# A transformer block with conditioning, state space, attention and product-key experts: features by quarters, conditioning on TensorE beside the gates, value tiles in turn

## The chip, the cores and the metric

The kernel runs on one core of a Trainium2 chip. The metric is the device time of one execution in microseconds, as a median over runs. TensorE multiplies matrices, VectorE and ScalarE work element by element, GpSimd (POOL in the profile) does so too and issues the indirect transfers, SyncE (SP) issues most of the others. Sixteen DMA engines move data between HBM and the on-chip memory.

## What is computed

256 tokens of width 2048 go through one block, in float32. The conditioning vector `c` gives six rows of 2048 (shift, scale and gate of both halves), by one product with a 2048 x 12288 matrix.

```python
s1, sc1, g1, s2, sc2, g2 = split(silu(c) @ w_ada + b_ada, 6)
h = rmsnorm(x, norm1_g) * (1 + sc1) + s1
u, q, kv, gates = split(h @ w_in)            # 2048 -> 1024, 1024, 1536, 24
y = concat(rmsnorm(s5_mixer(u)) * beta_ssm, rmsnorm(nsa_attention(q, kv, gates)) * beta_attn)
x = x + g1 * (y @ w_out)
h2 = rmsnorm(x, norm2_g) * (1 + sc2) + s2
x = x + g2 * peer(h2)
return rmsnorm(x, final_g)

def peer(h):             # 16384 experts; 8 heads choose 16 each per token
    expert, gate = top16_of_products(h @ w_q, sub_k1, sub_k2)
    a = gelu(h @ exp_u[expert].T)
    return (gate * a) @ exp_v[expert]
```

(`rmsnorm(v, g)` stands for the norm and its weight; the reference writes these lines out.) Products must keep float32 accuracy.

## The kernel before

**Split products.** A float32 weight unit of 128x1024 (512 KB) is loaded into one of four raw buffers (`unit`, L79), rounded by ScalarE to a `hi` part and its rest `lo` taken by VectorE (`split`, L89). Each product is then three fast ones: hi with hi, hi with lo, lo with hi. There are two buffers for each part in the later stages.

**Order.** The builder writes the work in program order; a planner with a timeline of its own then places each engine's instructions, by priority and by when operands should be ready. An engine carries out its own list strictly in order, and so does each engine's list of transfers to issue. `issue_after` pins an instruction behind another, `high_priority` moves a group up.

**Front.** The weights of the conditioning come in units of one 128-row tile and 1024 columns. `cond_job` (L379) multiplies 16 units of one half of one row group with `silu(c)`, in four column groups of the array side by side, and `cond_end` (L401) turns the summed rows into columns with small products (`pscol`, L415). The halves of `h` (`h_half`, L430) take the conditioning of scale (j = 1) and shift (j = 0). The first half is loaded through 11 buffers before anything is projected; then 16 projection blocks (`win_block`, L511) with the first half of the depth run, mixed with the second half's conditioning through a ring of three buffers `adap`, and `h_half(1)` follows. Meanwhile GpSimd builds the tables of the state space mixer.

**Middle.** A plan of blocks (L475 to L510, each with a cost) does the rest of the projections, the recurrence and the compression, then heads, gated projection and output projection. `pump` (L452) puts in steps of the conditioning of g1, scale and shift of the second norm: one per 8 of planned cost (L872), then in `tick` (L972) at every second tick, from the 17th at every one. There are 48 steps of two units. The results are turned into columns `late = 6` pumps after a job's end. `h2` is formed from products with a diagonal matrix (L1022) and the conditioning columns.

**Experts.** All 16384 experts are computed: 128 up-projection tiles (`u_tile`, L1067) of two units and 48 products each give activations of 128 experts by 256 tokens in `SA` (88 tiles) and `SB` (40). Beside the first 25 the top-16 choice runs; the next 64 are mixed with `g_group` (L1186), two per tile, which builds the gates of two tokens from one-hot rows: VectorE makes them, GpSimd scales them, TensorE multiplies, and VectorE and GpSimd multiply them into the activations. Then each expert's row of 256 weights, with its number in column 256, is scattered (88 indirect transfers, L1302) to HBM, in the order of places (`places`, L1242): experts that only the first 128 tokens use, that both use, that only the second use. In the same loop `g2_job` (L1307) computes g2: 32 units, one VectorE multiply-add each (L1315), summed over partitions by four products at the end.

**Value tiles.** `todo` (L1464) lists 51 places of the first list and 23 of the second, in order. `ENDS` says which hold which token tile: 20 for the first only, 15 for both, 16 for the second only; in the second list 8, 7 and 8. `load_rows` (L1357) loads the sorted weights four tiles at a time (514 KB, two buffers), and gathers the 128 rows of `peer_v` (1 MB) through their indices into one of four buffers. `v_tile` (L1426) splits rows and weights and runs 12 products of 512 columns for each token tile. From the fifth tile on, one scatter of the second list follows each tile, 40 in all. At `turn` all engines meet for a branch (L1494) that handles counts outside `ENDS`. `finals` (L1435) scales by g2, adds and normalizes.

Of the kernel before, what the change touches and what calls it, by code (L numbers as in the profile page):

```python
# [8 lines left out]
F32 = mybir.dt.float32  # L9
# [32 lines left out]

POOL_PAIRS = (1, 5, 9, 13)
# [7 lines left out]
ENDS = ((20, 35, 51), (8, 15, 23))  # L51


def build(tc, A):
# [34 lines left out]
    def split(raw, n=1024, lo_engine=None):  # L89

        hi, lo = buf("hi"), buf("lo")
        nc.scalar.copy(hi[:, :n], raw[:, :n])  # L92
# [100 lines left out]
    hT, uT, qT = uq, uq[:, :8], uq[:, 8:]  # L193
# [159 lines left out]

    for tt in range(2):
# [6 lines left out]
        norm_transpose(hv, ss[:, 2:3], s5t, lambda k, ps, tt=tt: nc.scalar.copy(  # L361
            hT[:, k:k + 4, tt * 128:(tt + 1) * 128], ps), "pqs",
            lambda: psS.tile([128, 4, 128], F32, name="pst", tag="py", bufs=2))
# [10 lines left out]
    sel2 = base1.tile([128, 2], F32, name="sel2")  # L374
    nc.vector.memset(sel2, 0.0)
    for i in range(4):
        nc.vector.memset(sel2[32 * i:32 * i + 1, i % 2:i % 2 + 1], 1.0)

    def cond_job(j, h, tags, late=0):  # L379
        ps = psM.tile([128, 512], F32, name="cps", tag="cps", bufs=1)  # L380
        for kt in range(0, KT, 2):
            rs = []
            for k in (kt, kt + 1):
                p, tag, bufs = tags[k % len(tags)]
                src = A["w_ada"][k * 128:(k + 1) * 128, j * D + h * 1024:j * D + (h + 1) * 1024]
                rs.append(unit(src, p, tag, bufs))
            for g in range(4):
                k, q = kt + g // 2, g % 2
                nc.tensor.matmul(ps[32 * g:32 * g + 32, :], scz[:, k], rs[g // 2][:, q * 512:(q + 1) * 512],  # L389
                                 start=kt == 0, stop=kt == KT - 2)  # L390
            yield
        rows = base1.tile([128, 512], F32, name="rows", tag="rows", bufs=1)
        nc.scalar.copy(rows, ps)
        if late:
            finish.append([late, j, h, rows])
        else:
            cond_end(j, h, rows)
# [3 lines left out]
    def cond_end(j, h, rows):  # L401
        if j == 2:
            b = base1.tile([1, 1024], F32, name="row", tag="adap", bufs=3)
            nc.gpsimd.dma_start(b, A["b_row"][0:1, h * 1024:(h + 1) * 1024])
            for q in range(2):
                cs = slice(q * 512, (q + 1) * 512)
                ps = psM.tile([1, 512], F32, name="psr", tag="mm", bufs=1)
                nc.tensor.matmul(ps, sel2[:, q:q + 1], rows, start=True, stop=True)
                nc.vector.tensor_tensor(out=b[:, cs], in0=b[:, cs], in1=ps, op=OP.add)
            nc.gpsimd.dma_start(g1d[:, h * 1024:(h + 1) * 1024], b)  # L410
        else:
            i = {0: 0, 1: 1, 3: 2, 4: 3}[j]
            ps = psM.tile([128, 8], F32, name="pscol", tag="mm", bufs=1)
            for b in range(8):
                nc.tensor.matmul(ps[:, b:b + 1], rows[:, b % 4 * 128:(b % 4 + 1) * 128], sel2[:, b // 4:b // 4 + 1],  # L415
                                 start=b == 0, stop=b == 7)
            o = cond[:, i, 8 * h:8 * h + 8]
            nc.vector.tensor_tensor(out=o, in0=ps, in1=bada[:, j, 8 * h:8 * h + 8], op=OP.add)
            if j in (1, 4):
                nc.vector.scalar_tensor_tensor(o, o, 1.0, ng[:, j // 4, 8 * h:8 * h + 8],  # L420
                                               op0=OP.add, op1=OP.mult)
# [8 lines left out]
    def h_half(h):  # L430
# [1205 lines left out]
```

## Time and profile before

| | us |
|---|---|
| three runs | 1933.39, 1949.06, 3670.4 |
| median | 1949.06 |
| the profiled execution | 1938.97 |
| its span, first to last instruction | 1937.2 |

| busy in the span | TensorE | VectorE | ScalarE | GpSimd |
|---|---|---|---|---|
| us | 1780.6 | 1440.4 | 798.2 | 788.6 |
| share | 92% | 74% | 41% | 41% |

The DMA engines move 440.39 MB, 227 GB/s on average. Busy time of TensorE overlaps itself, since products are pipelined and their ends are modelled: its pace is better read from the number of products in a stretch. The mean granted TensorE clock is 0.964 of full speed. The stages by time: conditioning and first norm to 172 us, middle to 560, output projection and second norm to 668, top-16 choice to 918, gates to 1337, maxima for the places to 1410, scatters to 1610, value tiles to the end.

### The profile page before, as it was taken

To read this page: it belongs to the slowest core of one execution; us is meant where nothing else is said; L and a number is where in the kernel's file an instruction comes from. 1 tells how busy PE (TensorE), PEld (TensorE's weight loads), DVE (VectorE), ACT (ScalarE), POOL (GpSimd) and SP (SyncE) were. 2 spreads that over 40 slices of the span, in tenths; PEclk is the share of its full clock that TensorE was granted. 3 is DMA by queue.
4 is the path that set the end of the run, shared out by engine and by line. 5 is a ranking of instruction groups with operands and counts; after the bars stand their busy time and mean duration, and the time that the engine had idled before them with its cause. 6 is when DMAs were issued, how large, how long until landed. Compare 5 with 4: busy or idle time off the path is not lost. (4 is left out here: it accounts for less than half of the span.)

```text
span 1937.2 us, 32031 instructions
## 1 busy us (share of the span) xinstructions
PE 1780.6 (92%) x11928; PEld 1492.2 (77%) x11928; DVE 1440.4 (74%) x2716; ACT 798.2 (41%) x1286; POOL 788.6 (41%) x867
## 2 busy tenths in 40 slices
PE   5798999999999799999999999999988888899896
PEld 2475666567776499999999999999977886687674
DVE  2524998856754288888999999999866666756657
ACT  3222222148633244344444444444323334645554
POOL 5910333201001101111766677774056744756333
PEclk8799999999999899999999999999989998999998
DMA  9769457587658455555555555445589996978974
GB/s 384 275 221 331 168 173 255 186 293 252 223 191 295 159 180 176 184 174 162 161 169 164 164 161 156 158 155 164 181 271 293 291 358 244 365 274 276 360 284 163
DMA packets 115994, 440.39 MB, mean 227 GB/s; under 512 B 16037, under 2 KB 18789, under 8 KB 105846
## 3 DMA queue, kind: packets, MB, share of 16 engines
q1 hardware_dynamic: 89712, 322.41, 50.1%
q0 software_dynamic: 21968, 112.29, 16.0%
q10 hardware_dynamic: 4150, 3.56, 0.6%
q8 instruction: 96, 1.57, 0.3%
q14 instruction: 68, 0.56, 0.1%
HBM read 415.05 MB, written 23.15 MB: 226 GB/s over the span
## 5 line engine op out<-in xcount | busy, mean ns | idle before, releaser
L92 ACT CAST hi<-raw 128x1024 fp32r<-128x1024 f32 x385 | 403.3, 1048 | 708.1 <-PE pa L471 316.4
L93 DVE TENSOR_TENSOR lo<-raw,hi 128x1024 fp32r<-128x1024 f32 x382 | 517.3, 1355 | 197.9 <-ACT hi L92 180.2
L471 PE MATMUL pa<-hhi,lo 128*128 128x256 f32 x2048 | 592.3, 289 | 38.3 <-DVE lo L93 37.5
L471 PE MATMUL pa<-hhi,hi 128*128 128x256 f32 x2048 | 584.6, 285 | 7.5 <-ACT hi L92 7.3
L471 PE MATMUL pa<-hlo,hi 128*128 128x256 f32 x2048 | 583.7, 285 | 0.0
L471 PEld LDWEIGHTS pa<-hhi,lo 128*128 128x128 f32 x2048 | 396.1, 193 | 54.0 <-DVE lo L93 51.5
L471 PEld LDWEIGHTS pa<-hhi,hi 128*128 128x128 f32 x2048 | 396.3, 193 | 8.9 <-ACT hi L92 8.9
L471 PEld LDWEIGHTS pa<-hlo,hi 128*128 128x128 f32 x2048 | 396.4, 194 | 0.0
L1402 DVE TENSOR_TENSOR lv<-rv,hv 128x1024 fp32r<-128x1024 f32 x144 | 174.4, 1233 | 79.2 <-ACT hv L1401 78.3
L1200 POOL TENSOR_TENSOR mv<-o,gp 128x256 fp32r<-128x256 f32 x256 | 168.6, 679 | 121.6 <-DVE o L1197 95.6
L1401 ACT CAST hv<-rv 128x1024 fp32r<-128x1024 f32 x144 | 147.6, 1049 | 95.5 <-DMA rv<-in_peer_v,wt 47.2
L1197 DVE TENSOR_TENSOR o<-pT,iota 128x256 fp32r<-128x256 f32 (+1 forms) x256 | 160.7, 629 | 1.4 <-PE pgs L1203 1.0
L389 PE MATMUL cps<-adap,scz 128*32 128x512 f32 x544 | 133.1, 651 | 23.2 <-DMA adap<-in_w_ada 23.2
L471 PE MATMUL lin<-hhi,hi 128*128 128x256 f32 x480 | 143.1, 299 | 3.9 <-ACT hhi L1034 2.1
L471 PE MATMUL lin<-hlo,hi 128*128 128x256 f32 x480 | 140.3, 293 | 6.4 <-DVE hlo L438 5.1
L471 PE MATMUL lin<-hhi,lo 128*128 128x256 f32 x480 | 140.0, 292 | 0.0
L1218 POOL TENSOR_TENSOR SA<-SA,gs 128x50 f32<-128x50 f32 (+42 forms) x128 | 134.3, 1050 | 1.4 <-DVE gs L1211 1.4
L1371 POOL DMA_INDIRECT rv<-in_peer_v,wt x74 | 88.7, 1198 | 103.3 <-DVE lv L1402 53.8
L1302 POOL DMA_INDIRECT wc<-SA,slot x88 | 105.5, 1199 | 47.4 <-DVE slot L1294 23.0
L471 PEld LDWEIGHTS lin<-hhi,hi 128*128 128x128 f32 x480 | 93.8, 196 | 33.4 <-issue 21.8
L1118 POOL TENSOR_TENSOR eq<-eq,iff 128x512 f32<-128x512 f32 x16 | 30.0, 1896 | 212.4 <-DVE eq L1117 212.4
L471 PEld LDWEIGHTS lin<-hlo,hi 128*128 128x128 f32 x480 | 93.7, 195 | 19.8 <-issue 9.9
(433 smaller groups left out, 3053.3 us busy)
## 6 DMA issues: line engine op xcount, KB each, us to landing
raw<-in_peer_u SPq DMA_DIRECT2D x256, 512.0 KB, 3.5
adap<-in_w_ada SPq DMA_DIRECT2D x136, 512.0 KB, 4.8
raw<-in_w_in SPq DMA_DIRECT2D x48, 512.0 KB, 5.6
raw<-in_w_out SPq DMA_DIRECT2D x32, 512.0 KB, 4.3
raw<-in_peer_wq SPq DMA_DIRECT2D x32, 512.0 KB, 3.5
raw<-in_w_ada SPq DMA_DIRECT2D x32, 512.0 KB, 5.8
wt<-wc POOLq DMA_DIRECT2D x19, 514.0 KB, 6.7
raw<-in_cmp_w SPq DMA_DIRECT2D x16, 512.0 KB, 4.4
```

Of the source, the lines that this page charges most:

```text
L92: nc.scalar.copy(hi[:, :n], raw[:, :n])
L93: (lo_engine or nc.vector).tensor_tensor(out=lo[:, :n], in0=raw[:, :n], in1=hi[:, :n].bitcast(F32), op=OP.subtract)
L389: nc.tensor.matmul(ps[32 * g:32 * g + 32, :], scz[:, k], rs[g // 2][:, q * 512:(q + 1) * 512], start=kt == 0, stop=kt == KT - 2)
L471: nc.tensor.matmul(ps, w, a[:, kk], start=first and u == 0 and k == 0 and i == 0, stop=last and u == n - 1 and k == 7 and i == 2)
L1118: nc.gpsimd.tensor_tensor(out=eq, in0=eq, in1=bc(iff[:, half].unsqueeze(2), EQ), op=OP.mult)
L1197: nc.vector.tensor_tensor(out=o, in0=bc(pT[:, j, t:t + 2].unsqueeze(2), shp), in1=io, op=OP.is_equal)
L1200: nc.gpsimd.tensor_tensor(out=mv[:, :, j], in0=o2, in1=g, op=OP.mult)
L1218: nc.gpsimd.tensor_tensor(out=o, in0=o, in1=tmp[:, a0:m], op=OP.mult)
L1302: d = nc.gpsimd.indirect_dma_start(out=wcs[i], out_offset=bass.IndirectOffsetOnAxis(ap=ap, axis=0), in_=SB[:, m - NSA] if i else SA[:, m], ...
L1371: d = nc.gpsimd.indirect_dma_start(out=raw, out_offset=None, in_=A["peer_v"], in_offset=bass.IndirectOffsetOnAxis(ap=t[:, T:T + 1].bitcast ...
L1401: nc.scalar.copy(hi, raw)
L1402: nc.vector.tensor_tensor(out=lo, in0=raw, in1=hi.bitcast(F32), op=OP.subtract)
```

## The change

**Front.** The conditioning weights are laid out so that a unit holds 2 depth tiles by 512 columns, whole in HBM. `cond_job` now does a quarter of a row group (8 units), with one vector `sel4` in place of `sel2`. `h_quarter` replaces `h_half`; features 4 to 7 of the depth go to two tiles of their own. The first quarter's conditioning is 16 units. The 16 projection units then hold two blocks by four depth tiles each (`win_quarter`, weights `w_inq`), eight for the first quarter and eight for the second, with 26 steps of the other three quarters' conditioning between them. Two loads of the mixer move behind the twelfth of them.

**Pump.** The later conditioning is done in quarters too, a step per 6 of planned cost and one at every tick, and is turned into columns 2 pumps after its end.

**g2.** Its 32 units are loaded beside the gates, two at every fourth up-projection tile, and multiplied on TensorE with one column of `silu(c)`, in four column groups. `g2_end` adds the bias and stores the row. The multiply-adds and loads beside the scatters go.

**Value tiles.** The index column moves to column 128, between the two token tiles' weights, so the columns of one token tile and the index lie together. Each tile loads its own weights: 129 of 257 columns if one token tile needs them, 257 if both; six buffers. The order is `ORDER_A` and `ORDER_B`. The gelu and multiply of an up-projection tile beside the gates become two instructions where they cross column 128. Indices of the second list's scatters are made one at a time, each behind the last row split. The first six row and three weight casts are pinned behind the last up-projection cast. The first token tile's `finals` comes one tile after its last product, with three more tiles to go.

```diff
+EARLY = (1, 1, 1, 2, 1, 2, 1, 1), (2, 2, 2, 2, 2, 2, 2, 2)
+ORDER_A = "0000" + "0b1" * 15 + "01"
+ORDER_B = "00b001" * 2 + "bb1bb1b11" + "11"
+TURN = 12
...
+    def cond_job(j, q, tags, late=0):
         ps = psM.tile([128, 512], F32, name="cps", tag="cps", bufs=1)
-        for kt in range(0, KT, 2):
+        for kt in range(0, KT, 4):
             rs = []
+            for p2 in (kt // 2, kt // 2 + 1):
+                p, tag, bufs = tags[p2 % len(tags)]
+                rs.append(unit(A["w_ada"][j, q, p2], p, tag, bufs))
             for g in range(4):
+                nc.tensor.matmul(ps[32 * g:32 * g + 32, :], scz[:, kt + g],
+                                 rs[g // 2][:, g % 2 * 512:(g % 2 + 1) * 512], start=kt == 0, stop=kt == KT - 4)
...
-    ada = jobs(((2, 0), (2, 1), (4, 0), (4, 1), (3, 0), (3, 1)), ring, 6)
+    ada = jobs([(j, q) for j in (2, 4, 3) for q in range(4)], ring, 2)
...
+    def parts():
+        for q in range(1, 4):
+            for j in (1, 0):
+                yield from cond_job(j, q, ring)
+            h_quarter(q)
+    steps = parts()
+    for q in range(2):
+        for b in range(8):
+            win_quarter(b, outs[b], q)
+            for _ in range(EARLY[q][b]):
+                next(steps, None)
+            if (q, b) == (1, 3):
+                s5_load()
+                s5_craw(0)
...
-        for _ in range(int(spent / 8) - int(x0 / 8)):
+        for _ in range(int(spent / 6) - int(x0 / 6)):
             pump(1)
...
-        pump(1 if clock[0] % 2 or clock[0] > 16 else 0)
+        pump(1)
...
+    def g2_job():
+        for kt in range(KT):
+            rs = [unit(A["w_g2"][kt * 128:(kt + 1) * 128, h * 1024:(h + 1) * 1024])
+                  for h in range(2)]
+            for g in range(4):
+                nc.tensor.matmul(g2ps[32 * g:32 * g + 1, :], scol[:, kt:kt + 1],
+                                 rs[g // 2][:, g % 2 * 512:(g % 2 + 1) * 512], start=kt == 0, stop=kt == KT - 1)
+            yield
...
+    g2 = g2_job()
     while state["t"] < T:
         for _ in range(2):
             g_group()
+        if state["t"] % 16 == 0:
+            next(g2, None)
         u_tile()
...
-                if kt:
-                    nc.vector.scalar_tensor_tensor(ac, r, sc, ac, op0=OP.mult, op1=OP.add)
...
-            chunks[i, c] = pool.tile([128, 4, T + 1], F32, name="wt", tag="wt" + tag, bufs=1 if tag else 2)
+        wt = pool.tile([128, T + 1], F32, name="wt", tag="wt" + tag, bufs=2 if tag else 6)
+
+        cs = slice(128 if tts[0] else 0, T + 1 if tts[-1] else 129)
+        nc.gpsimd.dma_start(wt[:, cs], wcs[i][128 * j:128 * j + 128, cs])
         raw = pool.tile([128, D], F32, name="rv", tag="rv" + tag, bufs=2 if tag else 4)
...
-    todo = [(i, j) for i in range(2) for j in range(ENDS[i][2])]
+    todo = []
+    for i, order in enumerate((ORDER_A, ORDER_B)):
+        of = {k: [j for j in range(ENDS[i][2]) if tts_of(i, j) == t] for k, t in zip("0b1", ((0,), (0, 1), (1,)))}
+        todo += [(i, of[k].pop(0)) for k in order]
+    turn = len(ORDER_A) + TURN
...
-        if j == ENDS[1][1] + 1:
+        if todo[turn + n - 1] == (1, ENDS[1][1] - 1):
             finals(0)
```

## Rows read from the trace of the kernel before

**Rows 1.** Table of stages (from:to in us; busy us and instructions per engine; clock; DMA; GB/s)
```profile
0.00:80.00 80.00, 44.40 (x216) 19.15 (x217) 32.89 (x93) 22.51 (x38) 58.34 (x96) 0.77 0.91 355
172.00:560.00 388.00, 377.86 (x2373) 266.99 (x2372) 309.63 (x656) 149.92 (x288) 84.57 (x91) 0.98 0.66 224
918.00:1337.00 419.00, 407.74 (x3319) 398.13 (x3319) 415.55 (x828) 196.52 (x385) 297.45 (x384) 1.00 0.50 160
1410.00:1610.00 200.00, 167.07 (x1238) 159.17 (x1237) 125.39 (x147) 64.28 (x83) 117.73 (x103) 0.94 0.92 307
1610.00:1821.00 211.00, 191.35 (x788) 149.80 (x787) 137.28 (x180) 113.45 (x148) 124.00 (x104) 0.96 0.85 300
```

**Rows 2.** Timeline of the front (start, us, engine, line, operation; what ended the idle time)
```profile
64.09 3.57 PE L415 MATMUL pscol<-sel,rows 128*128 128x1 f32 x16 [0.74 <-ACT rows L393]
...
67.90 8.50 DVE L435 TENSOR_SCALAR uq<-uq,cond 128x256 f32<-128x256 f32 x8
...
162.94 1.95 PE L415 MATMUL pscol<-sel,rows 128*128 128x1 f32 x16 [0.74 <-ACT rows L393]
171.98 0.80 PE L471 MATMUL lin<-hhi,hi 128*128 128x256 f32 x2
```

**Rows 3.** Timeline of TensorE, conditioning products among projection products and in a pair
```profile
91.22 1.05 PE L389 MATMUL cps<-adap,scz 128*32 128x512 f32 x4
92.20 0.39 PE L471 MATMUL lin<-hlo,hi 128*128 128x256 f32 x1
...
127.64 1.06 PE L389 MATMUL cps<-adap,scz 128*32 128x512 f32 x8
```

**Rows 4.** Table of stages, 10 us of the weight stream
```profile
50.00:60.00 10.00, 4.65 (x34) 1.53 (x28) 3.73 (x3) 3.13 (x3) 9.68 (x8) 0.84 1.03 417
```

**Rows 5.** Second norm: instructions of two tiles (ns min/median/max, first to last start), then TensorE's timeline
```profile
L389 PE MATMUL cps<-adap,scz x128: 592/617/1062, 568.1 to 657.5; 128*32 128x512 f32 x128
...
L1022 PE MATMUL pst<-dg,x2b x32: 274/276/582, 621.9 to 634.5; 128*128 128x128 f32 x32
...
658.81 1.95 PE L415 MATMUL pscol<-sel,rows 128*128 128x1 f32 x16 [0.74 <-ACT rows L393]
662.87 0.58 PE L471 MATMUL lin<-hhi,hi 128*128 128x256 f32 x1 [2.11 <-ACT hhi L1034]
```

**Rows 6.** Up-projection products by stretch, the multiply-add, unit loads from 1410 to 1610
```profile
1350.00:1400.00 50.00, 50.00 (x412) 49.43 (x411) 3.02 (x8) 1.00 0.59 184
1410.00:1610.00 200.00, 165.02 (x1233) 158.84 (x1231) 9.73 (x26) 0.94 0.92 307
...
L1315 DVE SCALAR_TENSOR_TENSOR ac<-raw,scol,ac x30: 1267/1284/1287, 1414.6 to 1608.2; 128x1024 f32<-128x1024 f32 x30
...
raw<-in_w_ada SPq DMA_DIRECT2D x29, 512.0 KB, 5.9
```

**Rows 7.** Gates: up-projection products, VectorE's groups from 945 to 1345, a small instruction
```profile
1000.00:1300.00 300.00, 285.83 (x2183) 269.24 (x2183) 24.46 (x90) 1.00 0.50 160
...
L93 DVE TENSOR_TENSOR lo<-raw,hi 128x1024 fp32r<-128x1024 f32 x122 | 188.1, 1542 | 1.6 <-ACT hi L92 1.0
...
1150.24 0.21 DVE L1211 TENSOR_TENSOR SA<-pgs,gs 128x56 f32<-128x56 f32 x1
```

**Rows 8.** Value stage: first product, two stretches, GpSimd's wait, its weight loads
```profile
1618.36 1.19 PE L1422 MATMUL accv<-hv,wh 128*128 128x512 f32 x2 [3.04 <-DVE place L1279]
...
1640.00:1660.00 20.00, 16.61 (x64) 11.04 (x63) 14.12 (x17) 12.22 (x18) 14.76 (x14) 1.00 1.00 334
1720.00:1740.00 20.00, 20.00 (x90) 16.55 (x89) 10.85 (x12) 9.07 (x12) 9.33 (x7) 1.00 0.68 239
...
POOL rv L1371 <- DMA wt<-wc: 21.1, 4, 7.7
...
L1367 POOL DMA_DIRECT2D wt<-wc x19: 756/808/822, 1573.6 to 1885.8; - x19
DMA to landing us min/median/max: 4.1/6.7/9.8
```

More of the change, by code (lines that the diff above doesn't have):

```diff
@@ L402, in cond_end @@
         if j == 2:
[L403 to L409, printed above, removed]
@@ L410, in cond_end @@
-            nc.gpsimd.dma_start(g1d[:, h * 1024:(h + 1) * 1024], b)
+            b = base1.tile([1, 1024], F32, name="row", tag="adap", bufs=3)[:, :512]
+            cs = slice(q * 512, (q + 1) * 512)
+            nc.gpsimd.dma_start(b, A["b_row"][0:1, cs])
+            ps = psM.tile([1, 512], F32, name="psr", tag="mm", bufs=1)
+            nc.tensor.matmul(ps, sel4, rows, start=True, stop=True)
+            nc.vector.tensor_tensor(out=b, in0=b, in1=ps, op=OP.add)
+            nc.gpsimd.dma_start(g1d[:, cs], b)
@@ L411, in cond_end @@
         else:
             i = {0: 0, 1: 1, 3: 2, 4: 3}[j]
[L413 to L418, printed above, removed]
+            ps = psM.tile([128, 4], F32, name="pscol", tag="mm", bufs=1)
@@ L524, in build, with win_quarter @@
     dest.update({16 + b: qT[:, b] for b in range(8)})
-    early2 = jobs(((1, 1), (0, 1)), ring)
-    second = False
-    for b in range(16):
-        win_block(b, dest[b], (0,))
-        for _ in range(2 if b % 2 else 1):
-            if not second and next(early2, 0) == 0:
-                second = True
-                h_half(1)
-                W.limit, W.after = None, last["ada"]
+    def win_quarter(b, out, q):
+        ps = psL.tile([128, 2, T], F32, name="lin", tag="lin", bufs=2)
+        hi, lo = W.get()
+        for i in range(2):
+            for k in range(4):
+                c = slice((4 * i + k) * 128, (4 * i + k + 1) * 128)
+                for n, (w, a) in enumerate(((hi, hhi), (hi, hlo), (lo, hhi))):
+                    nc.tensor.matmul(ps[:, i], w[:, c], a[:, 4 * q + k], start=k == 0 and n == 0,
+                                     stop=k == 3 and n == 2)
+        if q == 0:
+            nc.scalar.copy(out, ps)
+        else:
+            nc.vector.tensor_tensor(out=out, in0=out, in1=ps, op=OP.add)
+    outs = [uT[:, 2 * b:2 * b + 2] for b in range(4)] + [kvT[:, 2 * b:2 * b + 2] for b in range(4)]
+    def parts():
[12 more added lines that the diff above has]
+                s5_craw(0)
+    for _ in steps:
+        pass
     v = nc.vector
@@ L1070, in u_tile @@
             return
-        us = [split(unit(A["peer_u"][m, i])) for i in range(2)]
+        us = [split(unit(A["peer_u"][m, i]), keep=m == NK - 1) for i in range(2)]
         ps = psA.tile([128, 512], F32, name="pa", tag="pa", bufs=2)
@@ L1346, in build @@
             sent += 1
-        for _ in range(1 + (sent % 16 == 0)):
-            next(g2, None)
         if state["m"] >= seen + 8:
@@ L1393, in build, with behind @@
     fresh = set()
+    firsts = [6, 3]
+    def behind(k):
+        firsts[k] -= 1
+        return tc.issue_after(last["cast"]) if firsts[k] >= 0 else ExitStack()
     def v_split(raw):
```

213 lines of the change are left out of this document (107 added, 106 removed).

## Prediction

> **What bounds the kernel now.** Start with the table of stages, which cuts the span where the work changes [rows 1]; it gives each engine's busy time and the share of the DMA engines. No single engine bounds the whole. Up to 80 us the DMA share is 0.91 and TensorE's granted clock averages 0.77: conditioning weights stream in and little else can start. From 172 to 560 us TensorE is busy 377.9 of 388 us. From 918 to 1337 us VectorE is busy 415.6 of 419 us, so that stage (the routing gates) belongs to VectorE, with TensorE close behind. From 1410 to 1610 us, the scatters, DMA has a share of 0.92 and every engine idles. From 1610 us on come the value tiles, with DMA and TensorE each the limit in turn.
>
> Then look inside. The timeline of the start [rows 2] shows what the first norm waits for: the column products of the first conditioning half start on TensorE at 64.09, eight feature instructions on VectorE run from 67.90 for 8.50 us, and only after the second half (column products at 162.94) does the full-depth projection go on at 171.98. At the second norm [rows 5] TensorE is done with the transposing products at 634.5 us, yet the last conditioning column products start at 658.81 and the first product on the new features at 662.87: the last conditioning weights are simply late. In the scatter stage 1233 products of the up-projection take 200 us, where just before 412 took 50 us [rows 6]. In the value stage 20 us hold 90 products in the both-token stretch [rows 8], which is TensorE's own pace, 0.222 us each.
>
> **Front, by quarters.** A weight unit is 128x1024 f32, 0.524 MB; at the 417 GB/s of the stream [rows 4] it takes 1.26 us. The first features now need 16 units, not 32: 16 x 1.26 = 20 us earlier, so column products at 44 us instead of 64. Four feature instructions of 8.50/8 = 1.06 us and one pair of splits replace eight, so the projection starts near 52 us. The other 48 units (before: 32) are then mixed with 16 projection units of 24 products. One conditioning unit between projection products costs TensorE 92.20 - 91.22 = 0.98 us, and the restart runs 0.39 instead of 0.28, say 1.1 us [rows 3]; projection products follow each other every 50/412 = 0.12 us [rows 6]. TensorE therefore needs 384 x 0.12 + 48 x 1.1 = 99 us, and some 1.5 us for each of six more column-product sets, 9 us: 52 + 108 = 160 us, where before the last set started at 162.94. The features behind it are half as many, 6 us instead of 9, so the next projection is at 166 instead of 172: 6 us gained. If both units of a step arrive together, eight instructions take 1.06 us [rows 3], half as much per unit, and 26 us more go: 32 us. Units split apart were the usual case in this stretch, so I take the lower part: 12 us, ends 0 and 32.
>
> The rule that speaks against mixing small products in is in the Trainium skill, TensorEngine Tiling (Array Packing), Key Properties: changing the tiling mode drains the array. It agrees with the row, whose 1.1 us holds both switches; the page gives no price of its own, so the sum by it is unchanged.
>
> **Conditioning earlier.** The pump runs every 6 units of planned cost instead of 8, and at every tick. By the loop's own costs (186.7 in all) that makes 31 steps instead of 23 before the heads, and the 48 steps end at tick 17 instead of tick 33. So the 32 units (128 instructions, four each) that ran from 568.1 to 657.5 us [rows 5] leave that stage. Its end closes up from 662.87 to about 637 (the transposing products end at 634.5), 26 us, and some 20 of the units, 20 x 1.1 = 22 us, were TensorE work before 634.5. Together 48 us. The price is 35 us of TensorE time between 172 and 560 us, where it is 97% busy, though partly behind VectorE's recurrence. If nothing is hidden the net is 13 us, if all is, 48. I take 22, nearer the low end because of the 97%.
>
> **Last conditioning part.** The 32 fused multiply-adds on VectorE (1284 ns each, 30 in the trace [rows 6]) and 29 of 32 unit loads leave the scatter stage. There 1233 products at 0.121 us would take 150 of the 200 us, so 50 us are stall. Without 29 x 0.524 = 15.2 MB of loads the stage moves 307 x 0.2 - 15.2 = 46 MB; over 160 us that is 290 GB/s, less than the 307 of now [rows 1]. VectorE loses 39 us, and its subtraction no longer stands behind a multiply-add that waits for its own load. What is next is the scatter itself, 88 as before: GpSimd is busy 117.7 us in the stage [rows 1], under 150. I take 38, ends 20 and 50. Between the last up-projection product and the first value product four small products and two VectorE instructions go: 3 us.
>
> They come back beside the gates. A pass there takes 300 x 48/2183 = 6.60 us [rows 7]; TensorE needs 52 x 0.12 = 6.24, so it has 0.36 us to spare, 1.4 us in four passes, and VectorE has none (1.6 us of idle in front of 122 splits). A step of two units every fourth pass costs 1.1 us if they run together and 2.2 if not. Then 16 x (2.2 - 1.4) = 13 us is the least for units that run apart, and nothing for pairs; if the two-deep split buffers pass on every delay it is 35 us. A step also takes two of the four raw buffers, so the tile behind it loads with one tile of lead instead of two. The split output columns add one small instruction per tile; half of those, 32, are on VectorE, at most 0.21 us each [rows 7], 7 us. I take a loss of 16, near the least for units apart, ends 4 and 42.
>
> **Value tiles.** Before: 20 tiles for one token tile, 15 for both, 16 for the other, 12 or 24 products each. The first kind runs at DMA pace: 64 products in 1640 to 1660 us at a DMA share of 1.00 [rows 8], 3.75 us a tile where TensorE needs 2.66; the second at TensorE pace, 5.33 us. Taken in turn, three tiles (0, both, 1) need 48 x 0.222 = 10.7 us of TensorE and, at some 350 GB/s, 3 x 1.05 MB of rows, 0.4 of scatters and 0.27 of weights, 3.8 MB or 10.9 us. So 15 triples take about 11.4 us each, 171, and with the six other tiles 180 us, against 203 from the first product at 1618.36 [rows 8] to 1821, where the 788 products of the first list are done [rows 1]. In the second list 360 products are 80 us of TensorE against 91 now, of which the barrier keeps most: 3 us. The per-tile weight load costs GpSimd 0.81 us 74 times instead of 19, 45 us more in 327, on an engine that idles; but a gather stands behind its own weight load in GpSimd's order. I take off 6 for this: 20 us gained, ends -15 and 35.
>
> The order of the first splits behind the last up-projection cast costs nothing: ScalarE is busy 64 of 200 us there. The layout of weights in memory I also put at nothing, since the strided stream already runs at 417 GB/s.
>
> **The sum.** 12 + 22 + 38 + 3 - 16 + 20 = 79 us off the profiled span of 1937.2 gives 1858, and with the 1.8 us around it 1860. The profiled execution took 1938.97, within 0.6% of the median 1949.06 of the runs shown; the run of 3670.4 is used for nothing.
>
> **Rivals.** *More than the sum*: units run in pairs (32), the early conditioning hides fully (48), the scatters run at TensorE's pace (50), gates lose 4, values 25, with the 3: 154 us, 1785. For it: eight instructions in 1.06 us were seen. Against it: TensorE's 97%.
> *The cost only moves*: front 0, early conditioning 13, scatters 25, gates -35, values 10, with the 3: 16 us, 1923. For it: VectorE full in the gates and only two split buffers. Against it: TensorE has 0.36 us to spare in each pass.
> *GpSimd becomes the bound of the value stage, and the kernel slower*: each gather must wait for the load of its own tile's weights and indices. Four gathers of the trace waited 21.1 us for such a load [rows 8], 5.3 each. If no load is put ahead, a tile costs 0.81 + 5.3, 1.0 for the gather (priced like the load), and 0.6 on average for scatters and as much for gaps, 8.3 us; 74 tiles are 614 us instead of 307, or 2167 in all. It decides (over 2% slower, 1978) from (307 + 118)/74 = 5.7 us a tile, a wait of 2.7 us left over. Against it: six weight buffers stand beside four row buffers, so a load can be two tiles, 7 us, ahead.
> The Trainium skill, DMA: Bandwidth & Descriptors, Anatomy of one DMA, speaks against many small loads: each DMA that GpSimd issues pays about 2.0 us beside its bytes at 436 GB/s. A half load of 66 KB would then land in 2.15 us, an estimate, and with no load put ahead a tile would cost 5.2 us, the time be near 1935: no gain left, and no loss over 2%. The trace is slower than that rule: the loads of 514 KB, 3.2 us by it, landed in 6.7 in the median [rows 8], with gathers in flight before them.
>
> **How the numbers follow.** My sum has 0.55, with its own range from 1820 to 1900 (the ends of two or three terms together); more than the sum 0.15; the cost only moves 0.20; GpSimd the bound 0.10, of which 0.02 ends within 2%. A measurement of this kernel can tell about 2% from no change, so faster means under some 1905. The sum and the case above it give 0.70, and a third of the third case, with smaller losses, 0.08: 0.78. Same takes 0.12 and 0.02, 0.14. Slower 0.08. The range from 1795 to 1925 leaves out half of the second case, the last, and little else.
>
> **What would show it.** Right: column products of the first quarter near 44 us, the next full-depth projection before 166; no conditioning product after 560 us; the stage of the scatters near 160 us with VectorE under 90; passes beside the gates near 6.8 us; 15 triples near 11.4 us each, GpSimd waiting for weight loads under 40 us. Wrong: passes above 7.1 us, gathers that stand 3 us or more behind each load, or a gap before the second norm that is still there.

## The result and the profile after

The changed kernel takes 1907.93 us in the median of four runs (1904.61 to 1909.13), 0.9843 of the kernel before, 95% interval 0.9812 to 0.9873: some 31 us gained, where 79 were forecast and 1860 us predicted. It lies in the stated range (1795 to 1925) but not in that of the sum (1820 to 1900), near the rival "the cost only moves" (1923), and the gain of 1.6% is less than the 2% that the prediction asked of "faster". A second measurement beside the experiments gave 1906.71. The profiled execution has a span of 1905.4 us against 1937.2.

First the table of stages of the kernel after (from:to in us; busy us and instructions of PE, PEld, DVE, ACT and POOL; clock; DMA share; GB/s), to be held against [rows 1]:

```profile
50.00:80.00 30.00, 29.59 (x191) 21.44 (x191) 11.19 (x11) 9.41 (x13) 28.43 (x29) 0.91 0.71 245
80.00:100.00 20.00, 13.57 (x85) 7.37 (x81) 9.35 (x8) 4.63 (x7) 19.29 (x15) 1.00 0.85 303
...
160.00:180.00 20.00, 13.74 (x58) 3.21 (x58) 3.90 (x10) 1.82 (x3) 0.00 (x0) 1.00 0.83 283
...
920.00:1337.00 417.00, 410.98 (x3225) 377.37 (x3224) 380.31 (x832) 185.62 (x393) 290.40 (x377) 1.00 0.59 187
...
1440.00:1585.00 145.00, 144.57 (x1198) 143.75 (x1197) 79.03 (x102) 57.28 (x73) 111.33 (x104) 1.00 0.92 268
...
1600.00:1820.00 220.00, 207.89 (x877) 165.03 (x876) 155.69 (x233) 130.69 (x174) 153.96 (x154) 0.98 0.91 329
```

Three things have changed. TensorE now idles in the front (13.6 to 13.7 busy of 20 us, twice). Beside the gates VectorE is no longer full (380 of 417; before 416 of 419) and TensorE is (411). In the scatters TensorE is never waiting (144.57 of 145; before 167 of 200).

The views by tile give the ends of the stages. They are put side by side here, with all variants of the experiments below; times in us from the start of the span, each from the one profiled execution of its kernel. Up-projection products are those of the experts' activations, behind the second norm; placing products are the first of the work that finds each expert's place.

| kernel | first up-projection product | first gate product | first placing product | last up-projection product | first value product | last value product | span |
|---|---|---|---|---|---|---|---|
| before | 669.2 | 921.9 | 1404.2 | 1609.4 | 1618.4 | 1921.9 | 1937.2 |
| after | 665.7 | 920.6 | 1429.1 | 1584.5 | 1594.3 | 1887.9 | 1905.4 |
| after, second time | 667.6 | 921.2 | 1427.0 | 1582.4 | 1591.5 | 1884.4 | 1901.9 |
| e1, old conditioning pace | 689.4 | 946.9 | 1452.9 | 1633.5 | 1634.2 | 1925.1 | 1942.6 |
| e2, no last conditioning part | 666.5 | 920.6 | 1400.9 | 1584.7 | 1585.6 | 1875.1 | 1893.0 |
| e3, its loads alone | 667.9 | 920.6 | 1400.9 | 1580.6 | 1581.3 | 1872.0 | 1889.9 |
| e4, value tiles in old order | 666.2 | 921.0 | 1427.7 | 1608.2 | 1608.9 | 1917.9 | 1935.4 |
| e5, five buffers in the front | 654.8 | 908.3 | 1415.8 | 1571.2 | 1580.8 | 1873.0 | 1890.5 |
| e6, products in pairs | 659.8 | 913.3 | 1407.2 | 1589.0 | 1589.8 | 1882.5 | 1900.0 |
| e6b, pairs and five buffers | 628.0 | 881.4 | 1375.3 | 1530.7 | 1540.8 | 1834.6 | 1852.1 |
| e8, e4 and a fifth weight buffer | 665.7 | 920.7 | 1429.7 | 1593.4 | 1594.2 | 1908.5 | 1925.9 |
| e12, e6b and a fifth weight buffer | 629.7 | 884.2 | 1378.6 | 1542.9 | 1543.7 | 1834.6 | 1852.1 |
| b7, before without the last part | 669.8 | 922.4 | 1404.8 | 1582.7 | 1583.4 | 1891.5 | 1906.8 |
| b8, before, new conditioning pace | 652.5 | 906.3 | 1390.1 | 1592.4 | 1604.6 | 1907.7 | 1923.0 |
| b10, before, last part moved | 662.9 | 918.6 | 1426.5 | 1595.4 | 1596.2 | 1904.5 | 1919.7 |

The differences of its first two rows are the account of the change, stage by stage (gain in us, and what the prediction had put there). One more point divides the stretch before the second norm: the first full-depth projection product, which ends the front, at 171.98 before [rows 2] and 180.10 after. "Looks" are VectorE's searches for the maxima of finished activation tiles (`look`), from which the places follow.

| stretch | before | after | gained | forecast |
|---|---|---|---|---|
| start to the end of the front (first full-depth projection product) | 172.0 | 180.1 | -8.1 | 12 |
| to the second norm (first up-projection product) | 497.2 | 485.6 | 11.6 | 22 |
| to the first gate product | 252.7 | 254.9 | -2.2 | 0 |
| gates and looks (to the first placing product) | 482.3 | 508.5 | -26.2 | -16 |
| scatters (to the first value product) | 214.2 | 165.2 | 49.0 | 41 (38 and 3) |
| values and end of the span | 318.8 | 311.1 | 7.7 | 20 |
| together | 1937.2 | 1905.4 | 31.8 | 79 |

So 30 of the missing 47 us are lost before the second norm, 20 of them in the front, which is the first to look at. TensorE's timeline of the kernel after, where the projection products end and the last two sets of conditioning follow (start, us, engine, line, operation; in brackets the idle time before and what ended it), and one line of SP's queue:

```profile
151.55 1.05 PE L403 MATMUL cps<-adap,scz 128*32 128x512 f32 x4 [0.26 <-DMA adap<-in_w_ada]
154.39 4.26 PE L403 MATMUL cps<-adap,scz 128*32 128x512 f32 x12 [1.79 <-DMA adap<-in_w_ada]
...
165.90 1.05 PE L403 MATMUL cps<-adap,scz 128*32 128x512 f32 x4 [0.83 <-DMA adap<-in_w_ada]
167.78 1.05 PE L403 MATMUL cps<-adap,scz 128*32 128x512 f32 x4 [0.83 <-DMA adap<-in_w_ada]
169.66 1.05 PE L403 MATMUL cps<-adap,scz 128*32 128x512 f32 x4 [0.83 <-DMA adap<-in_w_ada]
...
174.88 1.05 PE L429 MATMUL pscol<-sel,rows 128*128 128x1 f32 x8 [0.74 <-ACT rows L407]
...
180.10 0.50 PE L482 MATMUL lin<-hhi,hi 128*128 128x256 f32 x2
...
144.97 33.54 SPq L91 DMA_DIRECT2D adap<-in_w_ada  x18
```

Here nothing but conditioning units is left to do. Each is worked off in 1.05 us, and then TensorE waits 0.83 us for the next: 1.88 us a unit, 18 loads in 33.5 us, though the stream brought one in 1.26 before [rows 4]. A unit can be asked for only when one of three buffers (the ring) is free. From 140 to 178 us a load landed 4.2 us after it was issued, in the median; with 1.05 of use that is 5.25 us for three buffers, or 1.75 a unit at best. The last column products start at 174.88, not at 160 as forecast, and 162.94 before [rows 2].

The other place is beside the gates. The last conditioning part as the tile view and the timeline show it, then waits from 920 to 1340 us (us in total, times, longest), the second from the kernel before, then the first look, before and after:

```profile
L1276 PE MATMUL psg<-raw,scol x128: 590/591/1061, 917.0 to 1343.8; 128*1 128x512 f32 x128
...
1000.05 1.03 PE L1276 MATMUL psg<-raw,scol 128*1 128x512 f32 x4
1003.74 0.40 PE L1248 MATMUL pgs<-mv,o 128*128 128x256 f32 x2
1004.30 1.03 PE L1276 MATMUL psg<-raw,scol 128*1 128x512 f32 x4
...
DVE o L1242 <- PE pgs L1248: 20.9, 26, 4.2
DVE o L1197 <- PE pgs L1203: 1.0, 2, 0.7
...
PE psg L1276 <- DMA raw<-in_w_g: 5.4, 8, 2.0
...
1341.69 2.28 DVE L1239 TENSOR_REDUCE mx<-SA 128x16 f32<-128x2048 f32 x1
...
1364.10 2.28 DVE L1308 TENSOR_REDUCE mx<-SA 128x16 f32<-128x2048 f32 x1
```

All 32 units stand alone, 1.03 us each but for one or two, and VectorE now waits 20.9 us for TensorE's gate products (before 1.0 us in all). The passes themselves did not grow: 64 of them take 414.5 us from the first gate product to the last (1335.1), where before it were 414.1. What TensorE owes is paid afterwards, as up-projection tiles left over, about four at the end of the passes: the first look starts at 1364.10, where before it did at 1341.69.

### The profile page after: what moved, and what is told of

It is laid out like the page before. It is cut to its first block, busy times and chain, and to the rows that moved or that the text cites. A ratio compares the mean times of both kernels' runs of the same rounds, so it can differ in the third digit from the quotient of the medians.

```text
span 1905.4 us, 32561 instructions
## 1 busy us (share of the span) xinstructions
PE 1789.0 (94%) x12048; PEld 1484.7 (78%) x12048; DVE 1382.6 (73%) x2765; ACT 799.9 (42%) x1325; POOL 815.4 (43%) x926
## 5 line engine op out<-in xcount | busy, mean ns | idle before, releaser
L482 PE MATMUL pa<-hhi,lo 128*128 128x256 f32 x2048 | 586.3, 286 | 4.4 <-DVE lo L102 4.0
L1245 POOL TENSOR_TENSOR mv<-o,gp 128x256 fp32r<-128x256 f32 x256 | 186.6, 749 | 127.3 <-DVE o L1242 65.7
L403 PE MATMUL cps<-adap,scz 128*32 128x512 f32 x592 | 144.1, 624 | 25.2 <-DMA adap<-in_w_ada 24.9
L1242 DVE TENSOR_TENSOR o<-pT,iota 128x256 fp32r<-128x256 f32 (+1 forms) x256 | 124.3, 500 | 33.9 <-PE pgs L1248 20.9
L1263 POOL TENSOR_TENSOR SA<-SA,gs 128x50 f32<-128x50 f32 (+42 forms) x128 | 113.8, 904 | 12.8 <-ACT SA L1120 12.4
L482 PE MATMUL lin<-hhi,hi 128*128 128x256 f32 x352 | 103.5, 295 | 1.9 <-ACT vN L737 0.8
L482 PE MATMUL lin<-hlo,hi 128*128 128x256 f32 x352 | 102.8, 292 | 2.2 <-ACT hlo L1065 1.4
L482 PE MATMUL lin<-hhi,lo 128*128 128x256 f32 x352 | 102.3, 291 | 0.0
L1253 ACT COPY gs<-pgs 128x256 f32<-128x256 f32 x128 | 47.6, 373 | 122.1 <-POOL SA L1263 107.7
L482 PEld LDWEIGHTS lin<-hhi,hi 128*128 128x128 f32 x352 | 67.9, 193 | 20.2 <-issue 12.9
```

Of the source, the lines that this page charges most:

```text
L403: nc.tensor.matmul(ps[32 * g:32 * g + 32, :], scz[:, kt + g], rs[g // 2][:, g % 2 * 512:(g % 2 + 1) * 512], start=kt == 0, stop=kt == KT - 4)
L482: nc.tensor.matmul(ps, w, a[:, kk], start=first and u == 0 and k == 0 and i == 0, stop=last and u == n - 1 and k == 7 and i == 2)
L1242: nc.vector.tensor_tensor(out=o, in0=bc(pT[:, j, t:t + 2].unsqueeze(2), shp), in1=io, op=OP.is_equal)
L1245: nc.gpsimd.tensor_tensor(out=mv[:, :, j], in0=o2, in1=g, op=OP.mult)
L1253: nc.scalar.copy(tmp, pv[:, 1])
L1263: nc.gpsimd.tensor_tensor(out=o, in0=o, in1=tmp[:, a0:m], op=OP.mult)
```

## The experiments

**The part beside the gates.** Three variants of the changed kernel leave out products, or loads and products, or set the products in another order. Without the part (`g2 = iter(())`, and the bias alone stored):

> The changed kernel without the last conditioning part (no loads, no products beside the gates; the gate of the last residual is the bias alone). It leaves that part of the computation out. Theory A, the prediction's term: 16 us, so gates and looks (first gate product to first placing product) take 492 instead of 508 us and the whole about 1892. Theory B: 32 units that run apart cost TensorE 32 x 1.05 = 34 us, of which about 10 were free; the stage falls to 482 to 484, the whole to about 1883. Theory C: the split output columns and the halved multiplies carry the loss; the stage stays above 496 and the whole above 1897.

With its loads alone (the loop of products taken out of `g2_job`, and the addition out of `g2_end`):

> The changed kernel with the loads of the last conditioning part kept beside the gates and its products left out (the gate of the last residual is the bias alone, so that part of the computation is missing). Gates and looks took 506 to 508 us with both, 480 with neither, 494 with products in pairs. Theory T (TensorE's time is the price): with loads alone 480 to 484. Theory L (two of the four weight buffers taken at each step make the next tile late): 488 to 494, the part that pairs left over.

And pairs, by the same edit in `g2_job` and in `cond_job`, here and in the other conditioning products:

```
-            for g in range(4):
+            for g in (2, 3, 0, 1):
```

> The changed kernel with one edit: of each pair of conditioning units the later one's products stand first, so that all four column groups run in one go (in program order the 32 units beside the gates now stand as 16 pairs, where the changed kernel has 32 singles; of the other conditioning products some 56 steps stand as pairs instead of 18). Theory B (the moved products cost TensorE one go each, 1.05 us, and it is the limit beside the gates and before the second norm): 16 goes fewer beside the gates, 17 us, and some 25 fewer before the second norm, 20 us where it is the limit: about 1875. Rival R: with three buffers in the ring a pair holds two of them until both have come, the front goes to the pace of the ring and loses 15 to 30 us there: 1890 to 1905. Theory C (the split columns set the pace of the gates): gates unchanged, 1890 or more.

Gates and looks took 480.3 us without the part, 480.3 with its loads alone, 493.9 with pairs and 508.5 as changed. So the loads by themselves cost nothing, and the products cost 28 us: 32 goes (a go is what runs side by side on the array) of 1.05 us are 34, TensorE waits 5.4 for their loads, and some 11 of these 39 fell into time that it had to spare. (Without a product to wait for, a load holds its buffer only until it has landed; what longer holding costs was not separated.) Pairs make 16 goes fewer, 17 us, and gave 14.6 back. e2 took 1895.22 us in the median, since its scatters were slower again (below), and e3 1891.69 in its only run, its scatters as slow. e6 took 1903.62. Its front lost what rival R had named, since with three buffers a pair is asked for only when two are free: the last column products came at 189.70, 14.8 later. Before the second norm this was made good (659.8, 5.9 ahead of the changed kernel), and 21.9 were gained by the first placing product; the slower scatters, 182.6 against 165.2, took 17.4 of that away. Its timeline in the front:

```profile
164.69 1.93 PE L403 MATMUL cps<-adap,scz 128*32 128x512 f32 x8 [3.45 <-DMA adap<-in_w_ada]
...
175.88 1.94 PE L403 MATMUL cps<-adap,scz 128*32 128x512 f32 x8 [3.72 <-DMA adap<-in_w_ada]
181.42 1.93 PE L403 MATMUL cps<-adap,scz 128*32 128x512 f32 x8 [3.61 <-DMA adap<-in_w_ada]
```

Two units come every 5.5 us, 2.8 each.

The same part moved in the kernel before, with the index column still at the end:

> The kernel before with one part of the change: the last conditioning part on TensorE beside the gates (same code as in the changed kernel; index column at the end, so no split columns). The prediction's terms: 16 lost beside the gates, 38 and 3 gained behind: 1914. By the runs so far: gates and looks 482 to 508 (26 lost), the scatter stage, 205 us, down to 178 to 181 as without the part in the kernel before or to 155 as in the changed kernel, and 6 to 9 us at the first value product: about 1930 with the one, 1905 with the other. If the split columns had a price beside the gates, the stage stays below 503.

Gates and looks took 507.9 us. So the split output columns of the changed kernel cost next to nothing (508.5 with them). The move alone took 1921.61 us, 0.992 of before (0.989 to 0.9951): 25.6 lost beside the gates, 44.5 gained in the scatters.

**The conditioning pace.** First undone in the changed kernel, `int(spent / 8)` for `int(spent / 6)`, the tick's `pump(1 if clock[0] % 2 or clock[0] > 16 else 0)` and 6 for 2 at the end of `ada`:

> The changed kernel with one part undone: the conditioning steps are issued at the old pace again (one per 8 units of planned cost instead of 6, every second tick, results taken 6 steps late). Theory A, the prediction's term: the earlier pace is worth 22 us, so this run takes about 1930 us (changed kernel: 1908). Theory B: the products cost TensorE their whole price wherever they stand, some 1.05 us per unit, and the gap before the second norm that they close is as large as the time they take earlier; then this run is within 8 us of 1908, its output projection ends some 30 us earlier, and the gap of some 25 us before the second norm is back.

It took 1953.63 us, which neither theory had: the second norm came 23.7 us later, and the scatters took 181.3 instead of 165.2. The old pace ended later here than in the kernel before (last conditioning product 680.9, there 657.5), so undoing it measures the pace together with what else was changed. The pace alone in the kernel before:

> The kernel before with one part of the change: the conditioning steps at the new pace (one per 6 units of planned cost, one each tick, results taken 2 steps late); the first norm by halves as before. Theory A, the prediction's term: worth 22 us; the first up-projection product, at 669.2 us in the kernel before, comes at about 647, the whole takes 1917. Then the front by quarters must have cost some 19 us in the changed kernel, where that product came at 665.7. Theory B (full price wherever TensorE is the limit): it stays within 5 us of 669 and the whole within 6 us of 1938; then the 24 us lost with the old pace in the changed kernel belong to the two parts together.

1923.28 us, 0.9913 of before (0.9885 to 0.9942). The first up-projection product came 16.7 us earlier. But 8.1 of these are there at the end of the front already, where the kernel before has 171.98 [rows 2]:

```profile
163.89 0.80 PE L471 MATMUL lin<-hhi,hi 128*128 128x256 f32 x2
```

The edit does not touch the front. b7 and b10, whose edits lie at the gates or behind them, have 169.18 and 165.15 there, so the front by halves ended at four times up to 8.1 us apart; the eight feature instructions of 8.50 us [rows 2] took 4.20 in b8 and 4.50 in b10. Behind the front b8 needs 488.6 us to the first up-projection product, 8.6 less than before; in the changed kernel the new pace needs 485.6 and the old one (e1, 689.4 - 180.9) 508.5, 22.9 more. The pace is thus worth 9 to 23 us, by what stands beside it. The front by quarters, which ends at 180.10, cost 8.1 us against the kernel before and 16.2 against b8.

**The front.** Two more buffers for its conditioning units, given back after it:

```
+    fr = ExitStack()
+    frp = fr.enter_context(tc.tile_pool(name="frp", bufs=1, side="right"))
+    wide = [ring[0], (frp, "adaf", 2)]
...
-                yield from cond_job(j, q, ring)
+                yield from cond_job(j, q, wide)
```

> The changed kernel with two more buffers in the conditioning ring of the front (five instead of three, the two given back after the front). Theory F (the front is paced by the ring: 18 units in 33.5 us, 1.86 us each, where the stream could bring one in 1.26): the last column product, at 174.9 us in the changed kernel, comes 20 to 30 us earlier, and the second norm's first product (665.7) about as much. Theory G (TensorE bounds the front, as the prediction had it): nothing moves by more than 5 us. If the gain of the front reaches the end, the whole takes about 1885; against the scatter stage of theory P, 1905.

1893.23 us, 0.9758 of before (0.9704 to 0.9813). The last column products start at 159.14 and the next full-depth projection at 166.49, where the prediction had 160 and 166, and the second norm comes 10.9 us earlier:

```profile
156.47 1.92 PE L403 MATMUL cps<-adaf,scz 128*32 128x512 f32 x4 [1.09 <-DMA adaf<-in_w_ada]
159.14 1.87 PE L429 MATMUL pscol<-sel,rows 128*128 128x1 f32 x8 [0.74 <-ACT rows L407]
...
166.49 0.79 PE L485 MATMUL lin<-hhi,hi 128*128 128x256 f32 x2
```

So theory F was right in kind, the ring paced the end of the front, and about half right in size (20 to 30 expected, 15.7 and 10.9 measured). The front by halves came to this point at 163.89 to 171.98 (above), so even with five buffers no gain of the quarters is shown. Pairs and five buffers together:

> The changed kernel with conditioning products in pairs everywhere (later unit's products first) and the five buffers in the front. Pairs alone: the gates' last pgs came 20 us earlier (1314.8 against 1335.1), 6 of it from ahead of the gates, but the front 4 us later, the ring being held by pairs. If the ring paced the front, pairs and ring together bring the second norm's first product 25 to 35 us before 665.7 and the first placing product to about 1375 (pairs alone 1407, changed kernel 1429); the whole is then 1870 to 1880. If TensorE did, the first placing product stays near 1405 and the whole near 1900.

1853.27 us, 0.9554 of before (0.9503 to 0.9605), which beats both kernels. The front ends at 160.57, and the second norm comes 37.7 us before that of the changed kernel, more than the 10.9 and 5.9 of each edit alone: pairs save TensorE's time only where the ring does not take it away again. The gates took 493.9, and the scatters kept their 165.5.

**The scatters.** The stretch from the first placing product to the first value product was read in every variant, though few of the edits touch it. In the changed kernel and its first variants it falls into two groups: 164 to 166 us (after twice, e5, e6b), the short pace, and 180 to 185 (e1 to e4, e6), the long one. The control:

> The changed kernel itself once more, beside the next three. In the four variants run so far the scatter stage (first placing product to last up-projection product) took 180 to 184 us, though none of them touches it; in the changed kernel's first profile it took 155. Theory P (the stage varies from run to run, by the place of the buffers or the chip): here it takes some 180 and the whole 1930. Theory Q (the stage depends on the order that the scheduler makes of the whole program): it takes 155 again and the whole 1908.

Theory Q: 164.5 again, and 1906.71 us. The kernel before without the last part:

> The kernel before without the last conditioning part (no loads, no multiply-adds; the gate of the last residual is the bias alone), which leaves that part of the computation out. The prediction's term: the scatter stage loses 38 us, ends 20 and 50, from 205 us (first placing product to last up-projection product): 167, and the whole 1899. Rival: the scatters alone hold the stage at 180, as in four variants of the changed kernel; then the stage is 180 and the whole about 1915.

178.6, and 1914.3 us: taking the part out is worth 35.6 us, and the other 13 of the 49 are put down to the short pace; with the part moved in the kernel before (b10) it was 169.7, between the two. ScalarE's casts of the up-projection weights show what the two are, first in e4 (idle time in front of the cast in brackets), then in the kernel after:

```profile
1480.43 1.05 ACT L99 CAST hi<-raw 128x1024 fp32r<-128x1024 f32 x1 [9.04 <-remote]
...
1509.09 1.05 ACT L99 CAST hi<-raw 128x1024 fp32r<-128x1024 f32 x1 [3.38 <-issue]
1514.25 1.05 ACT L99 CAST hi<-raw 128x1024 fp32r<-128x1024 f32 x1 [4.11 <-PE pa L482]
...
1543.09 1.05 ACT L99 CAST hi<-raw 128x1024 fp32r<-128x1024 f32 x1 [3.47 <-remote]
1548.26 1.05 ACT L99 CAST hi<-raw 128x1024 fp32r<-128x1024 f32 x1 [4.13 <-PE pa L482]
```

```profile
1477.50 1.05 ACT L99 CAST hi<-raw 128x1024 fp32r<-128x1024 f32 x1 [1.55 <-PE pa L482]
1480.38 1.05 ACT L99 CAST hi<-raw 128x1024 fp32r<-128x1024 f32 x1 [1.83 <-PE pa L482]
1483.26 1.05 ACT L99 CAST hi<-raw 128x1024 fp32r<-128x1024 f32 x1 [1.55 <-PE pa L482]
```

After: a cast every 2.88 us, all through. e4: at the longest hole ScalarE stands 9.04 us, and GpSimd then 4.82 us for its next places; shorter holes follow at 1509.09, 1543.09 and 1571.51, 28 to 34 us apart. Each of the five traces of the long pace has one such stall (9.04 to 10.14 us) and shorter ones; in the four of the short pace no wait in front of a cast is above 2.8. The traces of the long pace hold no landing times for the weight loads. But by the order of loads and casts, the unit cast at 1509.09 was asked for at 1498.0, 11.1 us before, and the one at 1480.43 at 1460.2, 20.2 us before; in the kernel after a load landed in 5.9 us in the median and in 10.2 at most, and at its pace four buffers leave some 9 (asked for at 1462.6, cast at 1471.74). If the hole is a weight load that comes too late for four buffers, a fifth should close it:

```
-        us = [split(unit(A["peer_u"][m, i]), keep=m == NK - 1) for i in range(2)]
+        us = [split(unit(A["peer_u"][m, i], *(state["rx"] if "rx" in state and (2 * m + i) % 5 == 4 else ())), keep=m == NK - 1)
+              for i in range(2)]
...
+    state["rx"] = (gq, "rx", 1)
```

> The sequential-order variant (scatter stage 180 us, with stalls that come back every 34 us, up-projection weight loads late by up to 9 us) with one weight buffer more during the scatters: five instead of four, so a load may come 2.9 us later before anyone waits. Theory L (late loads that find too little lead start and keep the slow course): the stage goes to 155 to 163 and the whole to 1915 to 1922. Theory S (the scatters themselves, or their order against the splits, set the pace): it stays at 178 to 182, and the whole at 1940.

164.5 instead of 181.2 in the same stretch, and from 1448 to 1588 us 166 to 169 products in each 20 us, where e4 had 78 to 168; in the whole 1929.68 us, 10.6 fewer than e4 (the value tiles took 5.3 more). The stage does what theory L expects; the whole lies between L's 1922 and the 1940 of theory S. It is not proof, since the pace also changed with edits elsewhere, and each was tried in one program. In the best variant, which had the short pace already, the fifth buffer gained nothing:

> Pairs everywhere and five buffers in the front (1853 us) with the fifth weight buffer during the scatters. Its scatter stage already took 155 us, where 1198 products at 0.121 us are 145. Theory L and S alike: within 5 us of 1853. If the fifth buffer turns the stage to the slow course, 1878.

1856.16 us, stretch 165.1. What decides which pace a program falls into was not found: e4's edit lies behind this stage.

**The value tiles** in the old order (`"0" * 20 + "b" * 15 + "1" * 16`, `"0" * 8 + "b" * 7 + "1" * 8`, `TURN = 10`):

> The changed kernel with the value tiles of each list in the old order (all of token tile 0, then those of both, then token tile 1; barrier after the second both-token tile again), all else as changed, the loads of one tile included. Theory A, the prediction's term: the order in turn is worth 26 us of the stage, this run takes about 1934. Theory B: the order is worth about 12 us, what the first list gained in the trace, and the rest of the forecast was never there: about 1920. Theory C: the order is worth nothing and the gain of the value stage is the half rows: 1908 within 4.

1940.23 us, level with before (1.0021, 1.0 to 1.0043). Of the 32 us against the changed kernel 16 are the scatters' pace. From the first value product to the last it is 309.0 against 293.6: the order is worth 15.4, nearest to theory B, and the old order with the loads of one tile costs 5.5 more than the kernel before (303.5).

## Why the prediction missed

It had the signs right but for the front's, and the sizes of the other terms wrong. Of the 47 missing us the front makes 20, the earlier conditioning 10, the gates 10 and the value tiles 12; the scatters gave 8 more than forecast.

**Front by quarters: 12 forecast, -8 measured at the end of the front (180.10 against 171.98; -16 against b8).** This is the step that failed. The first half of it held: column products of the first quarter at 41.37 us (44), the projection at 50.41 (52). The failing step is "TensorE therefore needs 99 us", and behind it 9: it counts TensorE's work and lets nothing else run late. From 50 to 180 us TensorE was busy 111.9 of 130 us. TensorE's waits for conditioning units are 10.9 us, many of them the 0.83 in front of a unit at the end, and those for features 8.1. The very row that gave 1.26 us a unit [rows 4] was taken while the units went into many buffers; the timeline [rows 2, 3] showed units from the ring of three alone, and no step asked how fast three buffers can turn over. e5 shows it: with five, 159.14 against the forecast 160. That it comes so near is partly chance, for TensorE waits 8.3 us for units there too, which the sum does not hold. Halving the sets made more of the front depend on the ring: 48 units instead of 32. And the 172 that the gain was counted from is the latest of the four fronts by halves.

**Conditioning earlier: 22 forecast, 11.6 measured behind the front (497.2 against 485.6).** Right in kind, and below its lower end of 13; b8 has 8.6 in the same stretch, 16.7 with its front, and e1 22.9. Why the size differs so was not tested. The forecast that no conditioning product runs after 560 us was wrong (the last starts at 611.4), yet the gap before the second norm was gone all the same.

**Beside the gates: -16 forecast, -26 measured.** The units ran apart, as assumed, and 16 x 2.2 = 35 is what they took. The cover was mis-sized: 0.36 us a pass makes 23, but the row of the stage had TensorE busy 407.74 of 419 [rows 1], so 11 were free. 35 - 11 = 24 would have been the forecast. That TensorE took VectorE's place as the bound was not said, nor that the debt falls due after the gates. The split columns, 7 us in the reasoning, cost next to nothing (b10), and the loads in the raw buffers nothing by themselves (e3). The Trainium skill, TensorEngine Tiling (Array Packing), Key Properties, says that different tiles can execute at once. The traces agree: four instructions on two column groups took 1.05 us in the kernel before, eight on four 1.06 [rows 3]. The prediction priced pairs at both places and took units apart as given; e6 shows that the order of four products decides it, and is worth 14.6 us beside the gates, where the move as a whole gained 18.9 (44.5 - 25.6 in b10).

**Scatters: 41 forecast, 49 measured.** Right in kind: the stage runs at TensorE's pace, 1198 products in 145 us at 0.121, with VectorE at 79 us. About 36 is the part's removal (b7); the rest is put down to a pace that a variant may also miss, as e1 to e4 and e6 did. In that the forecast was helped by chance.

**Value tiles: 20 forecast, 7.7 measured.** The triples were right: 664 products start from 1610 to 1770 us, 13.8 triples of 48, or 11.6 us each (11.4 forecast). What was wrong is the sum next to it: six tiles for one token tile got 9 us, but their 72 products are 16 us at TensorE's pace and 22 at the 3.75 us a tile that the prediction itself used. 171 + 22 = 193 would have been the forecast, and the last of the 792 products of the first list started 195 us after the first. By e4 the order is worth 15.4, where 23 and 3 were forecast. The loads of one tile at 6 (5.5 by e4) were right, and GpSimd waited 8.2 us for them, where up to 40 were allowed: the rival of a bound by GpSimd was never near. The Trainium skill, DMA: Bandwidth & Descriptors, Anatomy of one DMA, would have a half load of 66 KB land in 2.15 us, an estimate from its figures; in the scatter stage the first five landed in 5.0 in the median, slower than the rule, and no wait to speak of came of it.

The rival "the cost only moves" came closest, with 16 us in the sum; it had the front at nothing, and put the scatters at 25 (49 measured) and the gates at -35 (-26 measured).

## What to carry to other kernels

In this kernel the stretch in which small weight units are mixed into other work had three rates, that of the engine, that of the stream and that of the ring (buffers over load time and use). Read all three before such a stretch is forecast, and before a set is cut smaller. Where two half-filled products can share the array, set them so that the later load's product stands first, and give the loads buffers enough for a pair to arrive: with three the front lost 14.8 us by it, with five it gained. What an engine has to spare in a stage is nearer to its idle time in the stage's row (11 us here) than to a pass minus a count of products (23). A point in the trace ahead of every edit tells how far two kernels differ by themselves: the front by halves came out up to 8 us apart.

## What was not expected of the hardware

The stage in which loads and scatters share the DMA engines has two paces with the same loads and scatters: 155 us and 180 to 184 from the first placing product to the last up-projection product. In the long one ScalarE's casts stand once for 9.04 to 10.14 us (five programs) and for 3 us and more several times besides. By the whole times each program kept its own (e4 in ten runs 1936 to 1952 us, the changed kernel in eight 1904 to 1910), so an edit in one stage can move another by 25 us. One buffer more (e8) went with the return of most of it; the cause stays open.

The same eight feature instructions of VectorE took 8.50 us in one build of the front by halves [rows 2] and 4.20 in another (b8). No run here shows why.
